# Six input buffers, mix tiles of two units, and the last fifteen units transposed by the crossbar, in a gated token-mixing kernel

## The chip, the core and the metric

The kernel runs on one core of a Trainium2 chip. The core has a matrix engine (TensorE: PE for its matmuls, PEld for its weight loads), a vector engine (DVE), an activation engine (ACT), a general engine (POOL) and a queue engine (SP), each with its own in-order stream of instructions, and 16 DMA engines that they share. The metric is the device time of one execution in microseconds; the median of several executions is compared.

## The reference

```python
x_prev[:, 1:, :] = x[:, :-1, :]              # x_prev is 0 for the first token of a batch
xv = x * time_mix_v + x_prev * (1 - time_mix_v)
xr = x * time_mix_r + x_prev * (1 - time_mix_r)
v = xv @ value_weight
r = xr @ receptance_weight
out = (sigmoid(r) * v) @ output_weight
```

`x` has 16 batches of 2048 tokens with 256 features in float32; the four weights used here are 256 x 256 or vectors of 256. The key branch of the reference does not reach the output.

## The kernel before

**Units.** A batch of 2048 tokens is cut into 4 units of 512 tokens, which makes 64 units. Unit g belongs to batch g // 4. A batch from number 2 on is loaded with one DMA from POOL's queue (`load`, L109), which turns float32 into bfloat16, into a buffer `x_bf` of 128 partitions, 16 tokens each. There are five such buffers.

**Transposes.** The products need the features on the partitions. `transposes(i)` does this for unit i with 8 matmuls against an identity (L203) into `ps_t`, and ACT copies the result to `xt` (L219). A batch's `xt` has 17 slots of 128 columns: slots 1 to 16 hold its tokens, and slot 0 holds the predecessors of slot 1's tokens, that is slot 16 moved by one column. The last unit of a batch is therefore transposed first, and `wrap_slots` copies slot 16 to slot 0 on DVE (L413). Some units go another way: `by_dma` (L182) has SP issue one transposing DMA, which sends `x_bf` through the crossbar into `xt`. In the kernel before these are one unit in batch 4, one in batch 8 (`MID_T`), one in batch 12, and the three whole batches 13, 14 and 15. The one in batch 12 waits for the last input load besides its own.

**Mixing.** The weights are scaled by the mixing vector once, so that a mixed operand is c * x_prev + x. The product with c goes to DVE (L255), POOL (L265) and, late in the kernel, ACT (L495), half of the features at a time; DVE does the sums (L277). From unit 10 on a product covers two units. The results stand in `mix`, in two buffers of one batch each.

**The loop.** For each unit g, PE does 4 matmuls into `psum_r` (L285, called R here), then possibly the transposes of unit g + 6, then 4 matmuls into `psum_v` (V), then 8 matmuls of the output of unit g - 1 into `psum_o` (L309, O). ACT takes the sigmoid of `psum_r` (L516), copies the transposes, and copies `psum_o` to `o_sb` (L341). DVE multiplies sigmoid and `psum_v` to `z_sb` (L553). `psum_r`, `psum_v` and `psum_o` have one buffer each, so V of unit g + 1 waits until DVE has read V of unit g. SP stores two units at a time (L319, L344); the order of work on each engine is the order in which the program writes it.

**Stages.** `NU - BYDMA` is 51: units 1 to 50 are transposed on PE except for the two of `MID_T`. `CROSS` is 45, from where PE transposes nothing. From there one product of each pair of units goes to ACT instead of DVE. The transposing DMAs of batches 13, 14 and 15 are issued when g is 45, 47 and 51. The first units are prepared with 38 filler matmuls (`warm_up`), with unit 0 transposed from float32 in two halves, and with two transposes more for slot 0 of unit 0. The load of batch b + 4 is issued when batch b begins to be transposed.

The lines that the change touches are the constants at L48 to L68, `load`, `transposes`, `first_transposes`, `mixed`, `output`, `advance` and the loop from L502 on.

Of the kernel before, what the change touches and what calls it, by code (L numbers as in the profile page):

```python
# [8 lines left out]
FP32 = mybir.dt.float32  # L9
# [6 lines left out]
def kernel(  # L16
# [35 lines left out]
    LOOK = 6  # L52
    BYUNIT = 2
    H = UJ // 2
    BYDMA = 3 * UB + 1
    CROSS = NU - BYDMA - LOOK
    MID_T = (4 * UB, 8 * UB)
    START_T = [1, 3, 5, 6, 7, 9, 11, 12]
    AHEAD = 6
    PAIRS = 10  # L60
    WARM = 21
    WARM1 = 2
    WARM2 = 15

    consts = ctx.enter_context(tc.tile_pool(name="consts", bufs=1))
    xpool = ctx.enter_context(tc.tile_pool(name="xpool", bufs=5))
    xtpool = ctx.enter_context(tc.tile_pool(name="xtpool", bufs=3))
    mixpool = ctx.enter_context(tc.tile_pool(name="mixpool", bufs=2))  # L68
    zpool = ctx.enter_context(tc.tile_pool(name="zpool", bufs=3))
    opool = ctx.enter_context(tc.tile_pool(name="opool", bufs=3))  # L70
    ps_t_pool = ctx.enter_context(tc.tile_pool(name="ps_t", bufs=2, space=bass.MemoryType.PSUM))
# [28 lines left out]
    def load(b):  # L100
        if b not in x_bf:
            x_bf[b] = xpool.tile([P, J, D], BF16, name="x_bf")
        if b < BYUNIT:
            for e in range(UB):
                nc.gpsimd.dma_start(
                    out=x_bf[b][:, e * UJ : (e + 1) * UJ, :], in_=unit_rows(x, b, e)[:, 0]
                )
            return
        return nc.gpsimd.dma_start(out=x_bf[b], in_=rows(b), max_dma_last_dim=2048)  # L109

    x_unit = opool.tile([P, 3, UJ, D], FP32, name="o_sb")
    tm_rows = consts.tile([2 * KO, P], FP32)
# [62 lines left out]
        nc.vector.tensor_scalar(out=c_sb, in0=c_sb, scalar1=-1.0, scalar2=None, op0=ALU.add)  # L175

    coefficients()
    warm_up(WARM1)

    def by_dma(b, lo, hi, after=None):  # L180

# [7 lines left out]
    def transposes(i):  # L189

        b, e = divmod(i, UB)
        if b > 0 and e == 0 and b not in xt:
            new_xt(b)
        if b >= BYUNIT:
            e = (e - 1) % UB
        if UB * b in MID_T and e == 2:
            return
        j0 = 1 + e * UJ + (e if b < BYUNIT else 0)
        if b < BYUNIT or e == UB - 1:
            late_copies.append((b, e))  # L200

        def one(ps, jj, ko, src, idn):
            nc.tensor.transpose(  # L203
                out=ps[:, jj], in_=src[:, jj, ko * P : (ko + 1) * P], identity=idn
            )

        if i in (1, 2):
            for ko in range(KO):
                ps = ps_t_pool.tile([P, UJ, P], FP32, name="ps_t")
                for jj in range(UJ):  # L210
                    one(ps, jj, ko, x_unit[:, i], ident_f)
                nc.scalar.copy(out=xt[b][:, j0 : j0 + UJ, ko, :], in_=ps)
            return
        ps = ps_t_pool.tile([P, UJ, KO, P], BF16, name="ps_t")
        src = x_bf3 if b == 0 else x_bf[b][:, e * UJ : (e + 1) * UJ, :]
        for jj in range(UJ):
            for ko in range(KO):
                one(ps[:, :, ko], jj, ko, src, ident)
        nc.scalar.copy(out=xt[b][:, j0 : j0 + UJ], in_=ps)  # L219

    def first_transposes():
        def half(h, pool, name):
            ps = pool.tile([P, UJ, KO, P], FP32, name=name)
            for jj in range(H):
                for ko in range(KO):
                    nc.tensor.transpose(
                        out=ps[:, jj, ko],
                        in_=x_unit[:, 0, h * H + jj, ko * P : (ko + 1) * P],
                        identity=ident_f,
                    )  # L230
            nc.scalar.copy(out=xt[0][:, 1 + h * H : 1 + h * H + H], in_=ps[:, 0:H])

        pl = ps_t_pool.tile([P, KO, P], FP32, name="ps_t")
        for ko in range(KO):
            nc.tensor.transpose(
                out=pl[:, ko, 0:P], in_=x_unit[:, 0, UJ - 1, ko * P : (ko + 1) * P], identity=ident_f
            )
        nc.vector.tensor_copy(out=xt[0][:, 0, :, 1:P], in_=pl[:, :, 0 : P - 1])
        half(1, ps_r_pool, "psum_r")
        half(0, ps_v_pool, "psum_v")  # L240

# [5 lines left out]

    def mixed(piece):
        b, m, lo, hi = piece
        return mix[b][:, m, lo // P : hi // P]  # L250

    def scale(piece, kos=(0, 1)):
        b, m, _, _ = piece
# [27 lines left out]
    def project(ps, g, m, lo=0, hi=TU):  # L281
        b, e = divmod(g, UB)
        for mo in range(KO):
            for ko in range(KO):
                nc.tensor.matmul(  # L285
                    out=ps[:, mo, :],
                    lhsT=w_bf[:, m, ko, mo * P : (mo + 1) * P],
                    rhs=mix[b][:, m, (e * TU + lo) // P : (e * TU + hi) // P, ko],
                    start=(ko == 0),
                    stop=(ko == KO - 1),  # L290
                )
# [37 lines left out]
    def output(g, z):  # L329
# [1 line left out]
        if e == 0:  # L331
            o_sb[b] = opool.tile([P, J, D], FP32, name="o_sb")
        j0 = e * UJ
        if g >= NU - 3:
            for h, (pool, name) in enumerate([(ps_o_pool, "psum_o"), (ps_t_pool, "ps_t")]):
                out_part(pool, name, z, b, e, h * H, H, nc.scalar.copy, nc.sync)
            return
        ps = ps_o_pool.tile([P, UJ, D], FP32, name="psum_o")
# [3 lines left out]
        if b < BYUNIT:  # L342
            if e % 2 == 1:
# [1 line left out]
                    out=unit_rows(out, b, e - 1, 2),  # L345
                    in_=o_sb[b][:, j0 - UJ : j0 + UJ, :].rearrange("p (e j) d -> p e j d", j=UJ),
                )
        elif b == B - 1:
            store(nc.sync, b, j0, j0 + UJ)
        elif e % 2 == 1:  # L350
            store(nc.sync, b, j0 - UJ, j0 + UJ)
# [33 lines left out]
        out_part(ps_t_pool, "ps_t", z_sb, b, e, 3, 1, by_dve, nc.sync)  # L385

    def tile_for(b):
        if b not in mix:
            mix[b] = mixpool.tile([P, 2, J, KO, P], BF16, name="mix")

    def pieces(g):

        b, e = divmod(g, UB)
        tile_for(b)
        return [(b, m, e * TU, (e + 1) * TU) for m in range(2)]

    def wrap_slots(piece, one=None):
# [22 lines left out]
    def advance(limit):  # L420
        nonlocal tnext, last_load
        while tnext <= min(limit, NU - 1):
            b, e = divmod(tnext, UB)
            if b == 1 and e > 0:
                load(b + e + 1)
            elif b > 1 and e == 0 and b + 4 < B:
                last_load = load(b + 4)
            if tnext < NU - BYDMA:
                transposes(tnext)
            tnext += 1  # L430

    first_transposes()
    tile_for(0)
    for ko in range(KO):
        nc.vector.tensor_scalar(
            out=w_prev[:, ko, :],
# [62 lines left out]
                scale=c_sb[:, m, ko : ko + 1],  # L499
            )  # L500

    z_prev = None  # L502
    for g in range(NU - 1):
        ps_r = ps_r_pool.tile([P, KO, TU], FP32, name="psum_r")
        if g == 0:
# [8 lines left out]
            project(ps_r, g, 0)  # L514
        s_sb = zpool.tile([P, KO, TU], BF16, name="s_sb")
        nc.scalar.activation(out=s_sb, in_=ps_r, func=ACT.Sigmoid)  # L516
        if g == CROSS - 1:
            by_dma(B - 4, 2 * UJ, 3 * UJ, last_load)
        advance(START_T[g] if g < len(START_T) else g + LOOK)
        for b in range(B - 3, B):  # L520
            if g == max(UB * (b - 2) - 1, CROSS):
                new_xt(b)
                late_copies.append((b, UB - 1))
                by_dma(b, 0, J)
        if g + 2 * UB in MID_T:
            b = g // UB + 2
            new_xt(b)
            by_dma(b, 2 * UJ, 3 * UJ)
        for p in products.get(g + 1, []):
            if g >= CROSS and p[0][1] == 1:  # L530
                scale_act(p[0], (0,))
        for p in [q for q, _ in products[g]] + pooled[g]:
            last_unit_of = p[3] // TU - 1
# [4 lines left out]
        if g == 1:  # L538
            scale_act(pieces(2)[1], (1,))
        for p, kos in products[g]:  # L540
            if not (g - 1 >= CROSS and p[1] == 1):
                scale(p, kos)
        for p in sums[g]:
            last = add(p)
# [10 lines left out]
            scale_pool(p, last)  # L555
        for p in held[g]:
            add(p)
        if z_prev is not None:
            output(g - 1, z_prev)
        if g == 1:  # L560
            advance(4)
        z_prev = z_sb
    last_unit(NU - 1)


# [28 lines left out]
```

## Time and profile before

| what | value |
|---|---|
| median of 4 runs | 207.0 us (206.49 to 207.71) |
| the profiled execution's own time | 206.64 us |
| its span, from first to last instruction | 204.9 us |
| PE busy | 197.3 us (96%) |
| DVE busy | 189.1 us (92%) |
| ACT busy | 179.3 us (88%) |
| POOL busy | 86.0 us (42%) |
| input loads of a whole batch | 14, 932 ns to issue, 27.3 us median to landing (13.5 to 40.3) |
| stores of two units | 30, 7.5 us median to landing |
| granted TensorE clock | 0.9 or more of full speed in every slice |

A busy share is the sum of the durations of an engine's instructions, where overlaps count once; neighbouring instructions of one engine overlap by about 0.1 us, so a duration is longer than the distance to the next start. A row of the timeline gives start, duration, engine, line, operation, output and input, and in brackets the idle time before it and what ended it. Times below are counted from the span's start. An instruction that issues a DMA occupies its queue for the duration in its row; the transfer lands later.

### The profile page before, as it was taken

The numbers are of one execution on the slowest core, as the hardware profiler recorded it, in microseconds if no ns is written. First come the engines' busy times: TensorE is split into PE (matmuls) and PEld (weight loads), VectorE is DVE, ScalarE is ACT, GpSimd is POOL, SyncE is SP. The second block draws the span as 40 slices with busy tenths as digits, with TensorE's granted clock in tenths as the row PEclk, the third lists the DMA queues.
The fourth block names the chain that finished last, engine by engine and source line by source line (L and its number), as shares of the span: only waits on it lengthen the run. The fifth ranks groups of instructions, "written<-read, shape, count | busy, mean of one in ns | idle before, by whom it ended". The sixth has DMA issues, their size and how long they took to land.

```text
span 204.9 us, 3972 instructions
## 1 busy us (share of the span) xinstructions
PE 197.3 (96%) x1469; PEld 128.0 (62%) x1469; DVE 189.1 (92%) x308; ACT 179.3 (88%) x197; POOL 86.0 (42%) x109
## 2 busy tenths in 40 slices
PE   8999996999999999999999999999999999999992
PEld 7656664666666666666666666666655555555670
DVE  3899998999999999999999999999999999999962
ACT  3799897999899999999899999999988989898981
POOL 1864615253543545354264535434424444444200
PEclk9999999999999999999999999999999999999999
DMA  5999999999999999999999999999879999984385
GB/s 185 288 181 204 260 287 257 304 206 153 268 371 356 334 299 277 275 277 243 354 323 285 283 278 286 309 310 298 276 242 237 266 300 289 314 352 202 160 333 206
DMA packets 38379, 55.96 MB, mean 273 GB/s; under 512 B 16596, under 2 KB 32216, under 8 KB 35032
## 3 DMA queue, kind: packets, MB, share of 16 engines
q1 hardware_dynamic: 22656, 39.46, 56.0%
q0 software_dynamic: 15552, 16.12, 47.5%
q8 instruction: 11, 0.18, 0.3%
q10 hardware_dynamic: 152, 0.13, 0.2%
q14 instruction: 8, 0.07, 0.1%
HBM read 34.34 MB, written 33.55 MB: 331 GB/s over the span
## 4 chain that ended last, share of the span: by engine, by line
PE 70%; DMA 9%; ACT 8%; DVE 7%; issue 4%; POOL 1%; DVEq 0%; POOLq 0%
PE psum_v L285 20%; PE psum_o L309 19%; PE psum_r L285 17%; DMA x_bf<-in_x_dram 9%; PE ps_t L203 9%; ACT s_sb L516 5%; DVE z_sb L553 4%; PE ps_t L144 2%; ACT mix L495 2%; ACT o_sb L341 1%; DVE mix L277 1%; PE psum_r L299 1%; DVE mix L255 1%; POOL mix L265 1%; PE ps_t L309 1%
## 5 line engine op out<-in xcount | busy, mean ns | idle before, releaser
L265 POOL TENSOR_SCALAR mix<-xt,c_sb 128x1024 bf16<-128x1024 bf16 (+1 forms) x55 | 61.0, 1109 | 93.3 <-DVE mix L277 87.3
L553 DVE TENSOR_TENSOR z_sb<-s_sb,psum_v 128x1024 bf16<-128x1024 bf16 x63 | 76.7, 1218 | 4.1 <-PE psum_v L285 2.3
L277 DVE TENSOR_TENSOR mix<-mix,xt 128x1024 bf16<-128x1024 bf16 x112 | 77.3, 695 | 2.0
L341 ACT COPY o_sb<-psum_o 128x1024 f32<-128x1024 f32 x61 | 62.0, 1017 | 15.0 <-PE psum_o L309 14.8
L285 PEld LDWEIGHTS <-w_bf 128*128 128x128 bf16 x516 | 48.6, 98 | 38.4 <-issue 3.3
L285 PE MATMUL psum_v<-mix,w_bf 128*128 128x512 bf16 (+1 forms) x256 | 65.2, 377 | 0.7 <-DVE mix L277 0.2
L516 ACT ACTIVATE s_sb<-psum_r 128x1024 bf16<-128x1024 f32 x63 | 65.2, 1035 | 0.2 <-PE psum_r L299 0.2
L309 PE MATMUL psum_o<-wo_bf,z_sb 128*128 128x256 bf16 x498 | 64.8, 273 | 0.0
L285 PE MATMUL psum_r<-mix,w_bf 128*128 128x512 bf16 (+1 forms) x252 | 64.2, 377 | 0.0
L309 PEld LDWEIGHTS <-z_sb 128*128 128x128 bf16 x512 | 49.9, 98 | 19.8 <-DVE z_sb L370 0.8
L219 ACT COPY xt<-ps_t 128x1024 bf16<-128x1024 bf16 x41 | 41.6, 1026 | 0.8 <-PE ps_t L203 0.8
L203 PEld LDWEIGHTS <-x_bf 128*128 128x128 bf16 x368 | 24.0, 98 | 12.3 <-DMA x_bf<-in_x_dram 2.8
L203 PE MATMUL ps_t<-ident,x_bf 128*128 128x128 bf16 x368 | 27.6, 219 | 1.8 <-DMA x_bf<-in_x_dram 1.8
L255 DVE TENSOR_SCALAR mix<-xt,c_sb 128x1024 bf16<-128x1024 bf16 (+1 forms) x53 | 25.3, 486 | 0.0
L109 POOL DMA_DIRECT2D x_bf<-in_x_dram x14 | 13.1, 934 | 0.0
L277 DVE TENSOR_TENSOR mix<-mix,xt_first 128x1024 bf16<-128x1024 bf16 x15 | 10.2, 687 | 0.2 <-POOL mix L265 0.2
L495 ACT ACTIVATE mix<-xt,c_sb 128x1024 bf16<-128x1024 bf16 x8 | 9.2, 1149 | 0.0
L265 POOL TENSOR_SCALAR mix<-xt_first,c_sb 128x512 bf16<-128x512 bf16 x6 | 4.2, 697 | 7.8 <-DVE xt_first L413 7.8
L255 DVE TENSOR_SCALAR mix<-xt_first,c_sb 128x512 bf16<-128x512 bf16 x22 | 6.6, 348 | 0.2
L219 ACT COPY xt_first<-ps_t 128x1024 bf16<-128x1024 bf16 x5 | 5.1, 1018 | 0.0
L144 PE MATMUL ps_t<-zeros 128*128 128x128 bf16 x38 | 3.8, 275 | 1.0 <-DVE zeros L87 1.0
L144 PEld LDWEIGHTS <-zeros 128*128 128x128 bf16 x38 | 3.2, 125 | 1.0 <-DVE zeros L87 1.0
(65 smaller groups left out, 45.7 us busy)
## 6 DMA issues: line engine op xcount, KB each, us to landing
out_dram<-o_sb SPq DMA_DIRECT2D x30, 1024.0 KB, 7.5
x_bf<-in_x_dram POOLq DMA_DIRECT2D x14, 1024.0 KB, 27.3
x_bf<-in_x_dram POOLq DMA_DIRECT2D x5, 256.0 KB, 7.3
o_sb<-in_x_dram SPq DMA_DIRECT2D x2, 512.0 KB, 4.6
out_dram<-o_sb SPq DMA_DIRECT2D x4, 256.0 KB, 2.1
o_sb<-in_x_dram SPq DMA_DIRECT2D x2, 256.0 KB, 3.0
out_dram<-o_sb SPq DMA_DIRECT2D x1, 512.0 KB, 2.8
out_dram<-o_sb SPq DMA_DIRECT2D x3, 128.0 KB, 2.1
```

The costliest lines, as they stand in the source:

```text
L109: return nc.gpsimd.dma_start(out=x_bf[b], in_=rows(b), max_dma_last_dim=2048)
L203: nc.tensor.transpose(out=ps[:, jj], in_=src[:, jj, ko * P : (ko + 1) * P], identity=idn)
L219: nc.scalar.copy(out=xt[b][:, j0 : j0 + UJ], in_=ps)
L255: nc.vector.tensor_scalar(out=mixed(piece)[:, :, ko], in0=xt[b][:, slots(piece), ko], scalar1=c_sb[:, m, ko : ko + 1], scalar2=None, op0=A ...
L265: op = nc.gpsimd.tensor_scalar(out=mixed(piece)[:, :, 1], in0=xt[b][:, slots(piece), 1], scalar1=c_sb[:, m, 1:2], scalar2=1.0, op0=ALU.mul ...
L277: return nc.vector.tensor_tensor(out=mixed(piece), in0=mixed(piece), in1=xt[b][:, slots(piece, 1)], op=ALU.add)
L285: nc.tensor.matmul(out=ps[:, mo, :], lhsT=w_bf[:, m, ko, mo * P : (mo + 1) * P], rhs=mix[b][:, m, (e * TU + lo) // P : (e * TU + hi) // P, ...
L309: nc.tensor.matmul(out=ps[:, slot, :], lhsT=z[:, ko, jj * P : (jj + 1) * P], rhs=wo_bf[:, ko, :], start=(ko == 0), stop=(ko == KO - 1),)
L341: nc.scalar.copy(out=o_sb[b][:, j0 : j0 + UJ, :], in_=ps)
L495: nc.scalar.activation(out=mixed(piece)[:, :, ko], in_=xt[b][:, slots(piece), ko], func=ACT.Copy, scale=c_sb[:, m, ko : ko + 1],)
L516: nc.scalar.activation(out=s_sb, in_=ps_r, func=ACT.Sigmoid)
L553: nc.vector.tensor_tensor(out=z_sb, in0=s_sb, in1=ps_v, op=ALU.mult)
```

## The change

Sizes and counts: `BYDMA` goes from 13 to 15, so units 49 to 63 go by the crossbar and `CROSS` becomes 43; `MID_T` is gone, and PE transposes units 1 to 48 without exception. There are six input buffers instead of five, and the load of batch b + 5 is issued where that of b + 4 was. Each load is cut into pieces of 2048 float32 numbers instead of 512. `mix` has three buffers of two units instead of two of four.

Order: batch 12's transposing DMA now covers three units and is issued at g = 43, directly ahead of that of batch 13; those of batches 14 and 15 stay at g = 47 and 51. Slot 0 of batches 13 to 15 is filled by a DMA from SP (three of them) instead of a copy on DVE. From g = 44 on the output of unit g - 2 stands between R and V; before, the output of unit g - 1 stood after V. At g = 61 two outputs are written out. Units 56 to 59 are stored one by one, unit 60 in two halves, as units 61 and 62 were.

Start: seven filler matmuls and the two transposes for slot 0 of unit 0 are gone; DVE makes that slot from the first half's result.

```diff
-    BYDMA = 3 * UB + 1
+    BYDMA = 3 * UB + 3
     CROSS = NU - BYDMA - LOOK
-    MID_T = (4 * UB, 8 * UB)
+    FREE = CROSS
+    LATE_O = CROSS
-    WARM1 = 2
-    WARM2 = 15
+    WARM2 = 10
-    xpool = ctx.enter_context(tc.tile_pool(name="xpool", bufs=5))
+    xpool = ctx.enter_context(tc.tile_pool(name="xpool", bufs=6))
-    mixpool = ctx.enter_context(tc.tile_pool(name="mixpool", bufs=2))
+    mixpool = ctx.enter_context(tc.tile_pool(name="mixpool", bufs=3))
...
-        return nc.gpsimd.dma_start(out=x_bf[b], in_=rows(b), max_dma_last_dim=2048)
+        return nc.gpsimd.dma_start(out=x_bf[b], in_=rows(b), max_dma_last_dim=8192)
...
-    warm_up(WARM1)
...
-        if UB * b in MID_T and e == 2:
-            return
...
+            if h == 1:
+                nc.vector.tensor_copy(out=xt[0][:, 0, :, 1:P], in_=ps[:, H - 1, :, 0 : P - 1])
             nc.scalar.copy(out=xt[0][:, 1 + h * H : 1 + h * H + H], in_=ps[:, 0:H])
-        pl = ps_t_pool.tile([P, KO, P], FP32, name="ps_t")
-        for ko in range(KO):
-            nc.tensor.transpose(
-                out=pl[:, ko, 0:P], in_=x_unit[:, 0, UJ - 1, ko * P : (ko + 1) * P], identity=ident_f
-            )
-        nc.vector.tensor_copy(out=xt[0][:, 0, :, 1:P], in_=pl[:, :, 0 : P - 1])
...
-            mix[b] = mixpool.tile([P, 2, J, KO, P], BF16, name="mix")
+            mix[b] = mixpool.tile([P, 2, 2 * UJ, KO, P], BF16, name="mix")
...
-            elif b > 1 and e == 0 and b + 4 < B:
-                last_load = load(b + 4)
+            elif b > 1 and e == 0 and b + 5 < B:
+                if b == 2:
+                    load(6)
+                last_load = load(b + 5)
...
-        if g == CROSS - 1:
-            by_dma(B - 4, 2 * UJ, 3 * UJ, last_load)
+        if g == CROSS:
+            by_dma(B - 4, 0, 3 * UJ, last_load)
...
             if g == max(UB * (b - 2) - 1, CROSS):
                 new_xt(b)
-                late_copies.append((b, UB - 1))
                 by_dma(b, 0, J)
-        if g + 2 * UB in MID_T:
-            b = g // UB + 2
-            new_xt(b)
-            by_dma(b, 2 * UJ, 3 * UJ)
+                shifted = b
+        if LATE_O < g < NU - 2:
+            output(g - 2, z_prev2)
...
-        if z_prev is not None:
+        if z_prev is not None and not LATE_O <= g < NU - 3:
             output(g - 1, z_prev)
...
+        if shifted is not None and g == max(UB * (shifted - 2), CROSS + 1):
+            nc.sync.dma_start(
+                out=xt[shifted][:, 0, :, 1:P], in_=xt[shifted][:, J, :, 0 : P - 1]
+            )
```

## The prediction, made before the changed kernel was run

> **What bounds the kernel now.** I read the page's busy shares first (PE 96%, DVE 92%, ACT 88%: no engine has much room), then ACT's timeline, because the sigmoid (L516) starts when R of its unit is done and so marks each unit, then the rows of PE, DVE and SP where the distance between sigmoids departs from the rest.
>
> From unit 10 on, units with transposes on PE follow each other every 3.05 us (sigmoids at 43.57, 46.61, 49.66). The chain gives R, V and O 0.86, 0.86 and 0.87 us, and 8 transposes advance PE by 0.45: 3.04. Here **PE is the bound**. Units without transposes take 2.60 in the middle (52.71 to 55.31). Two places are worse than PE's own work.
>
> First, unit 7, whose sigmoid comes at 32.43 and whose successor's at 37.03. PE's and DVE's timelines there:
>
> ```profile
> 31.08 1.03 PE L285 MATMUL psum_r<-mix,w_bf 128*128 128x512 bf16 x4
> 33.73 0.62 PE L203 MATMUL ps_t<-ident,x_bf 128*128 128x128 bf16 x8 [1.62 <-DMA x_bf<-in_x_dram]
> ...
> 33.90 0.69 DVE L277 TENSOR_TENSOR mix<-mix,xt 128x1024 bf16<-128x1024 bf16 x1
> 35.32 1.22 DVE L553 TENSOR_TENSOR z_sb<-s_sb,psum_v 128x1024 bf16<-128x1024 bf16 x1 [0.73 <-PE psum_v L285]
> ```
>
> PE stands 1.62 us for batch 3's load; DVE only 0.73, because it was behind.
>
> Second, everything after the last transposes (sigmoid of unit 46 at 151.91, of unit 62 at 195.11): 16 units in 43.20, or 2.70 each, where PE needs 2.60. ACT's and DVE's timelines:
>
> ```profile
> 157.60 1.03 ACT L516 ACTIVATE s_sb<-psum_r 128x1024 bf16<-128x1024 f32 x1
> 158.51 1.15 ACT L495 ACTIVATE mix<-xt,c_sb 128x1024 bf16<-128x1024 bf16 x1
> 159.55 1.01 ACT L341 COPY o_sb<-psum_o 128x1024 f32<-128x1024 f32 x1
> 160.44 1.04 ACT L516 ACTIVATE s_sb<-psum_r 128x1024 bf16<-128x1024 f32 x1
> ...
> 161.52 1.22 DVE L553 TENSOR_TENSOR z_sb<-s_sb,psum_v 128x1024 bf16<-128x1024 bf16 x1 [0.30 <-ACT s_sb L516]
> ...
> 162.79 1.02 PE L285 MATMUL psum_v<-mix,w_bf 128*128 128x512 bf16 x4
> ```
>
> The reader is to see a ring: mix and copy hold ACT, the sigmoid starts late, z waits for it, and the next V waits for z, since `psum_v` is single.
>
> **Start: 0.** Gone are two float32 transposes (0.43 us of PE) and seven fillers. They stand ahead of the first real matmul at 6.04, which waits for `w_prev` on DVE (5.61, after 0.66 idle for the receptance weight's landing). If fewer fillers let PE's clock fall, the next 3.4 us (the early fillers ran 107 ns apart from 0.99 until about 4.4, then 56) would run at half speed: +1.7. The gap is only about 0.5 us, so I take 0. The other end, should a little come free, is -0.2.
>
> **Load: -1.3.** Of the trace's packet records on the loads' queue, those of 512, 1024 and 2048 bytes (as written) last 60, 98 and 173 ns: a line, 22 ns + 0.0735 per byte. A piece of 2048 numbers writes 4096 bytes: 323, against 4 x 98 = 392. A load falls from 1024 x 98 / 16 = 6.3 us of the 16 engines to 256 x 323 / 16 = 5.2. Batch 2 lands at 23.2 and batch 3 at 33.7, with DMA shares of 1.15 to 1.2, so full. Two loads save 2.2, and longer load packets should take a larger part beside stores (172 ns): batch 3 lands at about 30, before PE asks at 32.1. The Trainium skill (DMA: Bandwidth & Descriptors, Specifications) speaks against this: transfers from 512 bytes on already reach line rate. Then nothing is won and the stall stays. The line through three measured sizes says otherwise for this cast load; the size itself is extrapolated. The ends are 0 and -1.6; with PE's wait gone DVE is late next: z of unit 7 gains 0.73, later z's about 1.0, and PE can use up to 1.5 since V tolerates a late z. I take -1.3.
>
> The sixth buffer only issues loads 12 us earlier. After 34 us no transpose waits for a load, so that costs and gains nothing, except that all loads should have landed before 140 (the last landed at 146.2). POOL's issues get shorter, which is hidden in its 58% idle time. The mix tiles' reuse is five units after the last reader, as before: 0.
>
> **Middle: +0.9.** Units in batches 4 and 8 return to PE: 2 x 0.45, all on PE's path. The two crossbar transfers they replace ran beside loads (12.9 and 13.6 us to landing) and held SP 1.3 and 2.6, but nobody waited for them.
>
> **End: -2.0.** From the sigmoid of unit 43 (143.21) to that of 62 the time before is 51.90. After: 19 units x 2.60 = 49.4, without transposes. One bubble: O of unit 42 moves behind R of 44, so R 44 follows V 43 directly and waits 0.16 for the sigmoid. The order R, O, V gives ACT 0.87 more before z needs the sigmoid: behind copy and mix (0.91 each for sigmoid and copy, 1.04 for mix, in starts) the next sigmoid ends 3.9 after R of the unit before, and its V only 4.3 after. On DVE, starts lie 1.14 (z), 0.60 (sum) and 0.40 (product) apart, so z's are 2.74 apart with a product and 2.34 without, 2.54 in the mean: it keeps up with 2.60, barely. Ideal: -2.3. For jitter, 0.015 per unit, I take **-2.0**. The other end is the cadence of before, 2.70: -0.6. The displaced O's come back at unit 61, so their work is counted. Three DVE copies (0.13 each in starts) are hidden. The tail from 195 on is the same work: 0; more, smaller stores land in idle DMA.
>
> **Crossbar chain: +0.6, the largest doubt.** SP's timeline, and the landings of the last three:
>
> ```profile
> 149.94 7.16 SPq L182 DMA_TRANSPOSE xt<-x_bf  x1
> 157.19 0.53 SPq L319 DMA_DIRECT2D out_dram<-o_sb  x1
> 157.89 7.27 SPq L182 DMA_TRANSPOSE xt<-x_bf  x1
> 165.25 1.02 SPq L319 DMA_DIRECT2D out_dram<-o_sb  x2
> 166.44 9.29 SPq L182 DMA_TRANSPOSE xt<-x_bf  x1
> ...
> DMA to landing us min/median/max: 8.8/8.8/8.8
> ...
> DMA to landing us min/median/max: 10.8/10.8/10.8
> ...
> DMA to landing us min/median/max: 11.0/11.0/11.0
> ```
>
> In times of before (moved by what is won earlier): the store of unit 41 lets batch 12 start at 143.9. Three units, at three quarters of the rows, issue for 5.4 and land at 150.5 to 152.3; DVE's product at g = 46 wants them by 151.2, and a z may be late by 0.4 without harm. Batch 13 starts at 149.3 and lands at 158.1 to 160.1. Then comes what is new: SP waits for that landing to issue slot 0's DMA, and behind it stand the next store and batch 14. No row shows such a small copy inside SBUF; a 128 KB store (2.1 us) is nearest, the ends are 0.3 and 3.3 (the quickest transposing DMA). I take 2.1. Batch 14 starts at about 160, lands at 169 to 171, its slot 0 at 171.3 to 173.5, wanted at 172.1 (+0.4). Batch 15: start 170 to 172, slot 0 at 181 to 185, wanted at 182.5 (+0.4). In the fast case nothing waits; in the slow case the stalls at 12, 14 and 15 add up to about 3.7. The middle of the landings is some 0.6 late. By the skill (same page, Latency and other measured facts: 261 GB/s for a transposing DMA) a batch of 1 MB would take 4.0 us and never be late; the rows, 95 to 119 GB/s from issue to landing, decide. The held stores' buffers are not needed for 12 us or more.
>
> **Sum.** -1.3 + 0.9 - 2.0 + 0.6 = -1.8: profiled execution 206.64 to 204.8, span 204.9 to 203.1. That execution lies 0.4 below the median of 207.0, so the forecast of the median is 207.0 - 1.8 = **205.2**.
>
> **Rivals.**
> - *The crossbar chain decides* (slower). SP's waits serialize transfer, slot 0 and next transfer; landings of 11 us give +3.7 in place of +0.6: 207.0 - 2.4 + 3.7 = 208.3. For it: two of three landings at 10.8 and 11.0, and batches must follow every 10.4. Against it: loads are gone by then and batches 12 and 13 start earlier. It decides from an interval above 10.4 us between transposing DMAs of 14 and 15. Chance 0.18.
> - *The larger pieces bring nothing*: the stall of unit 7 stays. 207.0 + 0.9 - 2.0 + 0.6 = 206.5. Chance 0.15.
> - *DVE bounds the end*: the new order only moves the wait, cadence 2.70. 207.0 - 1.3 + 0.9 - 0.6 + 0.6 = 206.6. For it: DVE's 92%. Chance 0.12.
> - The forecast as summed, 203.8 to 206.0: 0.55.
>
> **How the numbers follow.** What can be told from no change is 0.5%, so 206.0 to 208.0 counts as the same. Of the forecast nearly all is below 206.0, with a little of the two middle rivals: faster 0.57. They and two fifths of the chain rival: same 0.29. Rest of the chain rival and the clock: slower 0.14. Range: below, all gains whole and no late transfer, 203.6; above, into the chain rival, 207.7.
>
> **What would show it.** Right: no PE row with a wait for `x_bf` near 32; sigmoids 3.05 apart throughout the middle, with no 2.60; 2.60 to 2.63 apart from unit 44 to 61; no wait of DVE, ACT or POOL for a transposing DMA or slot 0 above 1 us. Wrong: load packets near 390 ns; sigmoids still 2.70 apart at the end with DVE waiting for nothing; DVE's product at g = 46, 54 or 58 waiting for DMA by more than 1 us; matmuls after 6 us at twice the distance of before.

## The result, and the profile after

The changed kernel takes 206.21 us in the median of 41 executions (205.62 to 207.52), the kernel before 207.35 in 62 (205.55 to 209.63). The ratio of executions run side by side is 0.996, with a 95% interval from 0.9949 to 0.9972: faster by 0.4%, or about 0.8 us (1.14 by the medians), where 1.8 was forecast. The time lies inside the range. The profiled executions took 206.64 before and 205.75 after, with spans of 204.9 and 204.0.

The budget below is read from ACT's timeline: the start of the sigmoid of unit g is called s(g). The start of one execution can differ by more than a microsecond from that of the next, so a second profile of the kernel before stands beside the first.

| stretch | before | before, second profile | after | forecast of the change | after - before (first profile) |
|---|---|---|---|---|---|
| start to s(0) | 8.95 | 9.58 | 9.50 | 0 | +0.55 |
| s(0) to s(7) | 23.48 | 23.54 | 23.30 | 0 | -0.18 |
| s(7) to s(8) | 4.60 | 4.50 | 3.20 | -1.3 | -1.40 |
| s(8) to s(43) | 106.18 | 106.18 | 107.08 | +0.9 | +0.90 |
| s(43) to s(62) | 51.90 | 51.92 | 51.05 | -2.0 + 0.6 | -0.85 |
| s(62) to the span's end | 9.8 | 9.9 | 9.9 | 0 | +0.1 |

**Unit 7.** PE's timeline after, and DVE's z of unit 7, where PE had stood 1.62 us:

```profile
31.45 1.03 PE L279 MATMUL psum_r<-mix,w_bf 128*128 128x512 bf16 x4
32.31 0.61 PE L200 MATMUL ps_t<-ident,x_bf 128*128 128x128 bf16 x8
33.16 1.02 PE L279 MATMUL psum_v<-mix,w_bf 128*128 128x512 bf16 x4 [0.24 <-DVE z_sb L548]
...
35.02 1.20 DVE L548 TENSOR_TENSOR z_sb<-s_sb,psum_v 128x1024 bf16<-128x1024 bf16 x1
...
DMA to landing us min/median/max: 15.4/15.4/15.4
```

The last line is that of batch 3's load. The transposes follow R with no wait. Batch 3's load was issued at 15.2 and landed 15.4 later, at 30.6 (33.7 before). A wait of 0.24 for DVE's z is what is late next. Why the load came earlier is seen best in the DMA view of the stretch from 23.5 to 26.5 us, while the first store runs. Columns: queue, packets, MB, share of the 16 engines; q0 is the loads' queue, q1 SP's. First the kernel before, then the changed one:

```profile
q1 hardware_dynamic: 188, 0.77, 68.1%
q0 software_dynamic: 198, 0.20, 39.8%
```

```profile
q0 software_dynamic: 99, 0.41, 66.7%
q1 hardware_dynamic: 101, 0.41, 36.9%
```

Both have about as many packets of one queue as of the other: the engines take them by turns. Before, a load packet is 1,024 bytes and a store packet 4,096, so the loads get a fifth of the bytes (0.20 of 0.97 MB). Now both are 4,096 and the loads get half.

**The end.** ACT, DVE and PE at a place where nothing is late, the new order R, O, V:

```profile
161.79 1.02 ACT L513 ACTIVATE s_sb<-psum_r 128x1024 bf16<-128x1024 f32 x1 [0.61 <-PE psum_r L279]
162.71 1.01 ACT L335 COPY o_sb<-psum_o 128x1024 f32<-128x1024 f32 x1
163.60 1.16 ACT L491 ACTIVATE mix<-xt,c_sb 128x1024 bf16<-128x1024 bf16 x1
...
163.77 1.21 DVE L548 TENSOR_TENSOR z_sb<-s_sb,psum_v 128x1024 bf16<-128x1024 bf16 x1
...
164.19 1.04 PE L303 MATMUL psum_o<-wo_bf,z_sb 128*128 128x256 bf16 x8
165.06 1.03 PE L279 MATMUL psum_v<-mix,w_bf 128*128 128x512 bf16 x4
```

The ring is open: z no longer waits for the sigmoid (0.30 before), V no longer for z, and ACT has idle time of its own (0.61). Steps alternate between 2.86 and 2.34, the forecast 2.60 in the mean.

**Batch 12.** SP's timeline and three landings: those of batch 12, of batch 14, and of the first slot-0 copy.

```profile
143.73 10.94 SPq L181 DMA_TRANSPOSE xt<-x_bf  x2
156.62 0.70 SPq L558 DMA_DIRECT2D xt<-xt  x1
...
158.15 7.14 SPq L181 DMA_TRANSPOSE xt<-x_bf  x1
...
DMA to landing us min/median/max: 7.8/7.8/7.8
...
DMA to landing us min/median/max: 10.4/10.4/10.4
...
DMA to landing us min/median/max: 2.1/2.1/2.1
```

Issue and landing of batch 12 fell where they were put (143.9 and 150.5 to 152.3 in the prediction, 143.73 and 151.5 here), the first slot-0 copy took the 2.1 us assumed for it (the next two 2.4 and 2.8), and nobody waited for batches 13 to 15. But batch 12 was waited for. POOL's, DVE's and PE's timelines:

```profile
147.33 1.12 POOL L259 TENSOR_SCALAR mix<-xt,c_sb 128x1024 bf16<-128x1024 bf16 x1 [1.63 <-DVE mix L271]
151.72 3.00 POOL L259 TENSOR_SCALAR mix<-xt,c_sb 128x1024 bf16<-128x1024 bf16 x2 [3.28 <-DMA xt<-x_bf]
...
151.63 0.49 DVE L249 TENSOR_SCALAR mix<-xt,c_sb 128x1024 bf16<-128x1024 bf16 x1 [0.18 <-DMA xt<-x_bf]
...
153.77 2.09 DVE L271 TENSOR_TENSOR mix<-mix,xt 128x1024 bf16<-128x1024 bf16 x2
...
155.31 1.04 PE L279 MATMUL psum_r<-mix,w_bf 128*128 128x512 bf16 x4 [0.38 <-DVE mix L271]
```

DVE's product waited 0.18. POOL's product on the same slots could have begun at 148.44 and waited 3.28; then two of POOL's products stood in a row (3.00), DVE's sums came late (153.77), and s(46) to s(48) took 5.97.

### The profile page after: what moved, and what is told of

It is laid out like the page before. It is cut to its first block, busy times and chain, and to the rows that moved or that the text cites. A ratio compares the mean times of both kernels' runs of the same rounds, so it can differ in the third digit from the quotient of the medians.

```text
span 204.0 us, 3968 instructions
## 1 busy us (share of the span) xinstructions
PE 196.7 (96%) x1460; PEld 127.6 (63%) x1460; DVE 188.6 (92%) x304; ACT 180.0 (88%) x199; POOL 84.3 (41%) x109
## 4 chain that ended last, share of the span: by engine, by line
PE 73%; DVE 10%; DMA 7%; ACT 3%; issue 3%; POOL 1%; SPq 1%; DVEq 0%; POOLq 0%
PE psum_v L279 22%; PE psum_o L303 21%; PE psum_r L279 21%; PE ps_t L200 8%; DVE mix L271 4%; DMA xt<-x_bf 4%; DVE z_sb L548 3%; DMA w_f<-in_value_weight_dram 3%; DVE mix L249 2%; ACT s_sb L513 1%; ACT o_sb L335 1%; POOL mix L259 1%; PE ps_t L303 1%; ACT mix L491 1%; ACT xt L216 0%
## 5 line engine op out<-in xcount | busy, mean ns | idle before, releaser
L259 POOL TENSOR_SCALAR mix<-xt,c_sb 128x1024 bf16<-128x1024 bf16 (+1 forms) x55 | 61.8, 1123 | 92.9 <-DVE mix L271 83.9
L271 DVE TENSOR_TENSOR mix<-mix,xt 128x1024 bf16<-128x1024 bf16 x112 | 78.1, 704 | 1.9
L335 ACT COPY o_sb<-psum_o 128x1024 f32<-128x1024 f32 x60 | 61.1, 1018 | 7.8 <-PE psum_o L303 7.7
L249 DVE TENSOR_SCALAR mix<-xt,c_sb 128x1024 bf16<-128x1024 bf16 (+1 forms) x52 | 23.5, 459 | 0.2 <-DMA xt<-x_bf 0.2
L109 POOL DMA_DIRECT2D x_bf<-in_x_dram x14 | 10.5, 752 | 0.0
L491 ACT ACTIVATE mix<-xt,c_sb 128x1024 bf16<-128x1024 bf16 x9 | 10.4, 1160 | 0.0
L144 PE MATMUL ps_t<-zeros 128*128 128x128 bf16 x31 | 3.1, 281 | 1.0 <-DVE zeros L87 1.0
L209 ACT CAST xt_first<-ps_t 128x512 bf16<-128x512 f32 x4 | 2.1, 588 | 1.6 <-PE ps_t L200 1.6
```

The lines of the kernel that those rows point to most:

```text
L249: nc.vector.tensor_scalar(out=mixed(piece)[:, :, ko], in0=xt[b][:, slots(piece), ko], scalar1=c_sb[:, m, ko : ko + 1], scalar2=None, op0=A ...
L259: op = nc.gpsimd.tensor_scalar(out=mixed(piece)[:, :, 1], in0=xt[b][:, slots(piece), 1], scalar1=c_sb[:, m, 1:2], scalar2=1.0, op0=ALU.mul ...
L271: return nc.vector.tensor_tensor(out=mixed(piece), in0=mixed(piece), in1=xt[b][:, slots(piece, 1)], op=ALU.add)
L335: nc.scalar.copy(out=o_sb[b][:, j0 : j0 + UJ, :], in_=ps)
L491: nc.scalar.activation(out=mixed(piece)[:, :, ko], in_=xt[b][:, slots(piece), ko], func=ACT.Copy, scale=c_sb[:, m, ko : ko + 1],)
```

## The experiments

"Changed kernel" is the kernel after. Ratios are to the kernel before, run beside on the same chip; the changed kernel's own is 0.996.

**1. The start of before put back.** The two float32 transposes for slot 0 and all fillers return.

```diff
-    WARM2 = 10
+    WARM1 = 2
+    WARM2 = 15
...
+    warm_up(WARM1)
...
-            if h == 1:
-                nc.vector.tensor_copy(out=xt[0][:, 0, :, 1:P], in_=ps[:, H - 1, :, 0 : P - 1])
...
+        pl = ps_t_pool.tile([P, KO, P], FP32, name="ps_t")
...
+        nc.vector.tensor_copy(out=xt[0][:, 0, :, 1:P], in_=pl[:, :, 0 : P - 1])
```

> The changed kernel with the start of before: two transposes for slot 0 of unit 0 in a bank of their own, 38 fillers. Theory (ACT's copy of the first half waits for DVE's read of the same bank, which delays the first matmul): PE's wait for ACT at the first matmul (0.52 us) is gone, the first sigmoid comes near 9.0 instead of 9.5, and the kernel is 0.3 to 0.5 us faster than the changed one (about 205.8). Rival (the start's delay is absorbed later, or is a chance of one profile): the sigmoids of units 4 to 8 stand where they stood in the changed kernel and the time is unchanged within 0.2 us.

Measured: 206.70 us (22 executions), ratio 0.9978 (0.996 to 0.9995). So the new start is not seen to be slower; by the medians it gains 0.5, but the two intervals overlap.

Over the 19 profiles at full clock, of all kernels, s(0) lies between 8.95 and 12.98, and two things move it. The first is the landing of unit 1's input, whose DMA is issued at 2.15 in all of them: PE transposes unit 1 between the two halves of R of unit 0. It landed between 6.91 and 9.29, and in 15 of the 19 s(0) comes 2.03 to 2.09 after it, with the old start and with the new (before 6.91 and 8.95, after 7.46 and 9.50). That is the +0.55 of the budget.

The second is PE's rate. PE's timeline of the kernel before, and below it that of the first profile of experiment 2, which has the new start:

```profile
6.04 0.64 PE L299 MATMUL psum_r<-xt_first,w_prev 128*128 128x512 bf16 x2
6.55 0.61 PE L299 MATMUL psum_r<-xt_first,w_bf 128*128 128x512 bf16 x2
7.00 1.05 PE L203 MATMUL ps_t<-ident_f,o_sb 128*128 128x128 f32 x8
```

```profile
6.94 1.06 PE L293 MATMUL psum_r<-xt_first,w_prev 128*128 128x512 bf16 x2
7.79 1.06 PE L293 MATMUL psum_r<-xt_first,w_bf 128*128 128x512 bf16 x2
8.65 1.70 PE L200 MATMUL ps_t<-ident_f,o_sb 128*128 128x128 f32 x8
```

Here a pair of matmuls takes 1.06 us in place of 0.64 and 0.61, the sign that the prediction named, and s(0) comes 3.11 after the landing. Of the 16 profiles with the new start three are like this: 3.11, 2.83 (the fourth of experiment 5) and 3.68 (the third of experiment 12, where PE stands idle for 2.05 until the landing and then has a granted clock of 0.50 from 10 to 12 us). That is 0.8 to 1.6 us lost; in the other 13 it is 0.2 at most. None of the three profiles with the old start is like this, which is too few to say that the fillers prevent it, and the timing shows no gain from them.

**2. Batch 12's transfer one unit earlier.** Nothing else is changed.

```diff
-        if g == CROSS:
+        advance(START_T[g] if g < len(START_T) else g + LOOK)
+        if g == CROSS - 1:
             by_dma(B - 4, 0, 3 * UJ, last_load)
-        advance(START_T[g] if g < len(START_T) else g + LOOK)
```

> The changed kernel with batch 12's transposing DMA issued one unit earlier, at g = 42 behind the transposes and ahead of the store of unit 41. Theory (only batch 12's transfer is late; POOL's 3.3 us wait for it costs PE about 0.95): POOL's wait for the transposing DMA disappears, the sigmoids of units 46 to 50 are 2.60 apart in the mean, and the kernel is 0.8 to 1.0 us faster than the changed one (about 205.3). Rival (the chain as a whole is what binds): the wait moves to batch 13, 14 or 15 and less than 0.4 us is won.

Measured: 205.50 us (8 executions), ratio 0.9926 (0.9895 to 0.9958). SP's and POOL's timelines of this kernel:

```profile
139.26 5.97 SPq L181 DMA_TRANSPOSE xt<-x_bf  x1
...
151.50 1.12 POOL L259 TENSOR_SCALAR mix<-xt,c_sb 128x1024 bf16<-128x1024 bf16 x1 [1.43 <-PE psum_v L279]
```

The issue comes 4.5 us earlier, POOL's wait for the transfer is gone, s(46) to s(48) is 5.22, and s(43) to s(62) is 50.10 in place of 51.05. Batch 12's late landing cost 0.95 in the profile and about 0.7 in the time.

**3. The same once more,** for a better interval.

> The changed kernel with only batch 12's transfer issued one unit earlier, once more, since its first timing rested on 8 executions. Theory (the transfer's lateness costs 0.7 to 1.0): 205.2 to 205.7, ratio 0.990 to 0.994, units 43 to 62 in 50.1. Rival (that timing was favoured by chance, the transfer is worth nothing): 206.2, ratio 0.996.

Measured: 205.56 us (12 executions), ratio 0.9918 (0.9883 to 0.9953), and 50.10 again.

**4. The output's old place.** The output of unit g - 1 stands behind V again.

```diff
-    LATE_O = CROSS
+    LATE_O = NU
...
-        if z_prev is not None and not LATE_O <= g < NU - 3:
+        if z_prev is not None:
```

> The changed kernel with the output of unit g - 1 behind V to the end, as before. Theory (the order R, O, V takes ACT's late sigmoid out of the ring): the distance of sigmoids from unit 50 to 60 goes from 2.60 back to about 2.69 and the kernel is slower by 1.0 to 1.7 us (about 207.5). Rival (DVE has become lighter by the slot copies and sets 2.60 in either order): within 0.4 us of the changed kernel.

Measured: 207.51 us (22 executions), ratio 1.0023 (1.0003 to 1.0044), s(43) to s(62) 51.85. The new order is worth 1.3 us in the time. Past batch 12 the cadence shows it: s(50) to s(60) takes 26.75 here and 26.00 in the changed kernel. Batch 12's transfer is late in this kernel too, as POOL's timeline shows:

```profile
152.53 3.00 POOL L259 TENSOR_SCALAR mix<-xt,c_sb 128x1024 bf16<-128x1024 bf16 x2 [3.21 <-DMA xt<-x_bf]
```

So the new order is not what makes it late. The steps from s(47) to s(51) add up to 11.38, where the same four steps of the next period take 10.78: an estimate of 0.6 us for the delay with the old order. With the new order it costs 0.95, and where the transfer is in time (experiment 2) the stretch falls from 51.90 to 50.10, by 1.80.

**5. Load pieces of before.** The changed kernel with pieces of 512 numbers.

```diff
-        return nc.gpsimd.dma_start(out=x_bf[b], in_=rows(b), max_dma_last_dim=8192)
+        return nc.gpsimd.dma_start(out=x_bf[b], in_=rows(b), max_dma_last_dim=2048)
```

> The changed kernel with loads in pieces of 512 numbers, as before; six buffers stay. Theory (the larger pieces alone bring batch 3 in time): batch 3 lands after 33 us again, PE waits about 1.6 us for it, the step from unit 7 to 8 goes from 3.2 back to 4.6, and the kernel is slower by 1.2 to 1.6 us (about 207.6). Rival (the sixth buffer and the earlier issue do it): no PE wait, time unchanged. Third possibility: also the last load lands late, past 140, and batch 12's transfer waits for it, which would add up to 2 us more.

Measured: 207.47 us (14 executions), ratio 1.0013 (0.9991 to 1.0035), 1.26 above the changed kernel. Yet the profile showed no stall at unit 7 (step 3.35, batch 3 landed at 31.5). So three more profiles of it were taken.

> A second profile of the changed kernel with load pieces of 512 numbers. Theory (the larger pieces are worth 1.3 us because they take the stall at unit 7 away): in this profile the sigmoids of units 7 and 8 are 4.2 to 4.7 us apart, batch 3 lands after 33.0 us, and the first small-pieces profile, with no stall, was one of its quicker executions. Rival (the stall belongs to the kernel before, not to the piece size, and the small pieces lose their 1.3 us elsewhere): 3.0 to 3.4 us apart again.

> A third profile of the changed kernel with pieces of 512 numbers. The packet records say that loads move 63 KB per us beside a store and stores 256, so batch 3's load either ends just before the second store's packets start (31.5 in the two profiles so far, no stall) or some 3 us later (34.2 in the kernel with crossbar units, whose instructions are the same until then). Theory (a knife's edge, met or missed by chance): either a step of 3.35 with a landing at 31 to 32, or one of 4.4 to 4.9 with a landing at 34 to 35, and the stall in one of this and the next profile at least. Rival (the stall needs the crossbar units in the program): 3.35 in both.

> A fourth profile of the same kernel, with the same two theories: 3.35 and a landing at 31 to 32, or 4.4 to 4.9 and a landing at 34 to 35.

The second (207.89) and fourth (207.59) had steps of 3.35, the third (207.38) 4.38. PE's timeline in the third, and the landings of batch 3 in the third and the fourth:

```profile
31.82 1.04 PE L279 MATMUL psum_r<-mix,w_bf 128*128 128x512 bf16 x4
34.11 0.62 PE L200 MATMUL ps_t<-ident,x_bf 128*128 128x128 bf16 x8 [1.26 <-DMA x_bf<-in_x_dram]
...
DMA to landing us min/median/max: 18.6/18.6/18.6
```

```profile
DMA to landing us min/median/max: 14.7/14.7/14.7
```

The knife's edge stands, as the packet records of the third and fourth show. Loads move about 200 KB per us alone and 63 beside a store. In the third profile the second store's packets begin at about 29.5 us; by 30.0 the packets of 2.00 of the 2.10 MB of batches 2 and 3 had begun, and the rest crawled: landing at 34.1. In the fourth the second store begins at about 30.7, and by 30.0 load packets of 2.16 MB had begun, some of them batch 4's: landing at 31.4. All profiles, by piece size and start:

| load pieces | s(0) below 10 | s(0) from 10 on |
|---|---|---|
| 512 or 1024 numbers | 7 profiles, 6 with a step of 4.4 to 4.9 | 4 profiles, none |
| 2048 numbers | 3 profiles, none | 5 profiles, none |

In these profiles a late start lets the loads finish before the second store begins. So with small pieces an execution lost either at the start or, in 6 of 7, at unit 7; with large ones only at the start. The four profiles have s(0) to s(62) longer than the changed kernel's by 0.25 to 1.32, less in the mean than the 1.26 that was timed.

**6. A second look at the kernel before.**

> The kernel before, unchanged, for a second profile. Question: is the wait for batch 3's load at unit 7, and the first sigmoid at 8.95 us, a property of this kernel or of one execution? Theory (the stall is in nearly every execution, since the loads fill the DMA engines): PE again waits 1 to 2 us for batch 3 and the step from unit 7 to 8 is about 4.6. Rival (it comes and goes with how the first DMAs land): the step is 3.2 to 3.4 here and the whole time lies near 206.

Measured: 207.37 us, step 4.50 at unit 7.

**7. Large pieces in the kernel before.** Pieces of 2048 numbers, nothing else.

```diff
-        return nc.gpsimd.dma_start(out=x_bf[b], in_=rows(b), max_dma_last_dim=2048)
+        return nc.gpsimd.dma_start(out=x_bf[b], in_=rows(b), max_dma_last_dim=8192)
```

> The kernel before with the one edit of loads in pieces of 2048 numbers. Theory (larger pieces are worth about 1.2 us by themselves, as undoing them in the changed kernel cost 1.2): about 206.0, ratio 0.994, no PE wait for batch 3, the last load lands before 140. Rival (they only pay together with the sixth buffer): within 0.3 us of before.

Measured: 214.14 us in the median of five executions, ratio 1.0351 (1.0314 to 1.0388): 7 us slower where a gain was expected. A sixth, the profiled one, had a granted clock of 0.66 and took 297.91; in it batch 4's crossbar transfer landed after 12.8 us and nobody waited for it, so it does not show the reason. The next experiment makes one likely; for this kernel it is not shown.

**8. The middle's crossbar units put back,** with large pieces.

```diff
+    MID_T = (4 * UB, 8 * UB)
...
-        if b > 0 and e == 0:
+        if b > 0 and e == 0 and b not in xt:
...
+        if UB * b in MID_T and e == 2:
+            return
...
+        if g + 2 * UB in MID_T:
+            b = g // UB + 2
+            new_xt(b)
+            by_dma(b, 2 * UJ, 3 * UJ)
```

> The changed kernel with the two crossbar units of batches 4 and 8 put back, beside the loads; batch 12 still has three. PE transposes two units less. Theory (PE's work returned to the middle costs 0.9, and a crossbar transfer beside loads harms nobody): 0.8 to 0.9 us faster than the changed kernel, about 205.3, sigmoids of units 13 and 14 and of 29 and 30, or thereabouts, 2.60 apart. Rival (it delays loads or stores so that something waits): unchanged or slower, with a wait on DMA in the middle.

Measured: 219.65 us, ratio 1.0599 (1.0562 to 1.0635). SP's, POOL's, DVE's and PE's timelines, and the landing of batch 4's unit:

```profile
37.14 7.81 SPq L182 DMA_TRANSPOSE xt<-x_bf  x1
...
DMA to landing us min/median/max: 30.1/30.1/30.1
...
68.14 0.75 POOL L110 DMA_DIRECT2D x_bf<-in_x_dram  x1 [12.04 <-DMA xt<-x_bf]
...
70.13 0.69 DVE L274 TENSOR_TENSOR mix<-mix,xt 128x1024 bf16<-128x1024 bf16 x1 [10.37 <-POOL mix L262]
...
72.01 1.86 PE L282 MATMUL psum_v<-mix,w_bf 128*128 128x512 bf16 x4 [9.70 <-DVE z_sb L555]
```

One unit's transfer, which landed in 12.9 us before, takes 30.1. POOL's next load (L110) is to fill the input buffer that this transfer still reads, and waits for it 12.04; POOL's product stands behind that load, DVE waits for POOL, PE for DVE. In the kernel before, where the transfer landed at 54.5, POOL came to its load only at 55.4. The DMA view of 47 to 53 us, first of the kernel before, then of this one:

```profile
q0 software_dynamic: 734, 0.74, 88.1%
q1 hardware_dynamic: 735, 0.19, 40.7%
```

```profile
q0 software_dynamic: 289, 1.12, 96.1%
q1 hardware_dynamic: 289, 0.09, 12.1%
```

In both, one load packet goes for each packet of 256 bytes of the transposing DMA. With load packets of 4,096 bytes that leaves 289 transposing packets in 6 us instead of 735, of 1,024 that the unit has.

**9. The same with batch 12 early.** The edits of experiments 2 and 8 together.

> The changed kernel with both: batch 12's transfer one unit earlier, and the two crossbar units of batches 4 and 8 back. Theory (the two parts are independent and add): 206.2 - 0.8 - 0.9 = 204.5, ratio to before about 0.987. Rival (they are two names for one slack): no better than the better one of them, 205.3.

Measured: 218.67 us, ratio 1.0567 (1.0532 to 1.0602). The step from unit 16 to 17 is 17.30; s(43) to s(62) is 50.09. So the middle alone costs the 13 us.

**10. The same with pieces of 1024 numbers** (packets of 2,048 bytes, 173 ns), to see whether the effect grows with the packet.

```diff
-        return nc.gpsimd.dma_start(out=x_bf[b], in_=rows(b), max_dma_last_dim=8192)
+        return nc.gpsimd.dma_start(out=x_bf[b], in_=rows(b), max_dma_last_dim=4096)
```

> The kernel with batch 12's transfer issued earlier, the crossbar units in batches 4 and 8 put back, and load pieces of 1024 numbers (2,048-byte packets, 173 ns by the packet records). Theory of packets by turns: 64 transposing packets per engine times 18 + 173 ns make about 12 us of packets for batch 4's unit, landing some 8 us earlier than with the 4,096-byte packets, so the stall at unit 16 to 17 falls from 14 us to between 3 and 7, and the time to 207 to 212. Rival (a threshold between 1,024 and 2,048 bytes, no gradual effect): packets of about 20 us as with 4,096 bytes and a time of 218 to 220. If no wait at all is left there, 204.8.

Measured: 206.38 us (10 executions), ratio 0.9983 (0.9949 to 1.0017). Landing, DVE's and PE's timelines:

```profile
DMA to landing us min/median/max: 16.8/16.8/16.8
...
62.33 0.69 DVE L274 TENSOR_TENSOR mix<-mix,xt 128x1024 bf16<-128x1024 bf16 x1 [2.45 <-POOL mix L262]
...
64.21 1.02 PE L282 MATMUL psum_v<-mix,w_bf 128*128 128x512 bf16 x4 [1.66 <-DVE z_sb L555]
```

The first to the last of the unit's transposing packets start 12.2 us apart, where turns give 64 x (18 + 173) ns = 12.2. The step from unit 16 to 17 is 4.87, a stall of 1.82: less than the 3 to 7 expected. The mechanism came out to the number, the cost did not.

**11. The middle's crossbar units with pieces of 512 numbers.** The edits of experiments 5 and 8 together.

> The changed kernel with load pieces of 512 numbers and with one crossbar unit each in batches 4 and 8, so the end's changes on the middle and load of before. Theory (each DMA engine takes packets by turns from the loads and from the transposing queue, so that the 19.6 us of the transposing packets are the price of the 4,096-byte load packets): the packets of batch 4's unit run about 8 us, POOL waits under 1 us for them, no sigmoid step above 5 us but perhaps that of unit 7, and the time is that of the small-pieces kernel less 0.9: 206.6, ratio 0.996 to 0.999. Rival (the sixth buffer's earlier loads or the mix tiles of two units make that transfer late, whatever the piece size): a stall of over 5 us at unit 16 to 17 stays, and the time is above 212.

Measured: 207.39 us (12 executions), ratio 1.0025 (1.0001 to 1.0048). Of the mechanism all came true: packets over 7.7 us, no wait of POOL for them, and the two steps of 2.60 back in the middle (s(8) to s(43) 106.19 against 107.08). The time did not: unit 7 stalled (4.62), and s(43) to s(62) was 52.37: batch 12's transfer, which waits for the last load, started only at 146.53.

**12. That with batch 12 early.** The edits of experiments 2, 5 and 8 together; one timing and two more profiles.

> The kernel with batch 12's transfer issued earlier, with the crossbar units in batches 4 and 8, and with pieces of 512 numbers. By the theory of packets by turns the transposing packets of batch 4's unit last about 8 us and nobody waits for them, while batch 3's load is robbed by the stores again: 205.5 (earlier transfer, large pieces, no crossbar units) + 1.3 in executions where unit 7 stalls - 0.9 = 205.5 to 206.0, ratio 0.992 to 0.996, and in the profile units 17 to 18 and 33 to 34 of 2.6 us. Rival (the crossbar units cost elsewhere what they save on PE, as the 207.4 of the kernel with the late transfer and small pieces suggests): 206.5 to 207, ratio 0.998 to 1.001.

> A second profile of the kernel with small pieces, earlier transfer and crossbar units, whose timed executions lie 2.4 to 3.5 us above its first profiled one (205.89). Theory (in the usual execution the start is early, s0 near 9.7, the stores rob batch 3's load, and the crossbar transfer of batch 4, which waits for batch 4's load behind it, is late besides): a step of 4.4 to 4.9 at unit 7 and another stall of 1 to 3 us at unit 16 to 18, total 208 to 209.5. Rival (the first profile is the usual case and the timed ones lost their time in the end's transfers): no stall at 16 to 18, steps of over 3 us between units 43 and 61.

> A third profile of the same kernel, with the same two theories. Should it again be one near 205.9 with s0 near 11, the excess of the timed executions stays open.

Measured: 208.65 us in the median of 7, ratio 1.0079 (1.0053 to 1.0106), though the first of them, the profiled one, took 205.89. The second and third profiles are of 207.94 and 207.46. In the second, the one with an early start (9.49), SP's and POOL's timelines:

```profile
145.55 3.62 SPq L182 DMA_TRANSPOSE xt<-x_bf  x1
...
173.75 3.00 POOL L262 TENSOR_SCALAR mix<-xt,c_sb 128x1024 bf16<-128x1024 bf16 x2 [3.44 <-DMA xt<-xt]
```

Batch 12's transfer was placed as in experiment 2 but starts at 145.55 instead of 139.26, because it waits for the last load: the last load packet ends at 145.0 here, at 132.9 in experiment 2. All later transfers are late in turn, slot 0 of batch 14 by 3.44, and s(43) to s(62) takes 53.05. No stall came at unit 16 to 18, so that half of the first theory fell. The first and third profiles, with starts of 11.1 and 13.0, had 50.10 at the end. This shows one way to lose 3 us, not that it is what the timed executions lost; that stays open.

**13. ACT's copy of the first half ahead of DVE's slot-0 copy,** on top of experiment 2.

```diff
+            nc.scalar.copy(out=xt[0][:, 1 + h * H : 1 + h * H + H], in_=ps[:, 0:H])
             if h == 1:
                 nc.vector.tensor_copy(out=xt[0][:, 0, :, 1:P], in_=ps[:, H - 1, :, 0 : P - 1])
-            nc.scalar.copy(out=xt[0][:, 1 + h * H : 1 + h * H + H], in_=ps[:, 0:H])
```

> The kernel with batch 12's transfer issued one unit earlier, and besides ACT's copy of the first half ahead of DVE's copy into slot 0, which read the same tile: the changed kernel's first matmul from the first half waited for that ACT copy, which waited 2.07 us for DVE's at the start. Theory (the earlier transfer is worth 0.7, a copy that no longer waits at the start a little more): 205.0 to 205.5, ratio 0.989 to 0.993. Rival (the start ends on the first transfers' landing, not on the copies): 205.5, the same as with the earlier transfer alone, first sigmoid at 9.5 or later.

Measured: 205.19 us (9 executions), ratio 0.9946 (0.9912 to 0.9979). ACT's copy starts at 4.57, waiting for PE alone, but s(0) is still at 10.31, again 2.04 after the landing of unit 1's input: the rival held. By the ratios it cannot be told from experiment 2. The version to keep is that of experiments 2 and 3.

## Why the prediction was right, and where it was wrong

The step that failed is the crossbar chain: it looked at the wrong reader of batch 12's transfer, and the late transfer cost 0.95 us where the whole chain was given 0.6. The end was 0.2 too hopeful. What is left of the miss, 0.4 to 0.7 us, lies in the start, which was put at 0, or in how often the load's gain comes; that stays open.

**Base and start (0).** In the profiles s(0) to s(62) fell by 1.51 (186.14 in the second profile of before to 184.63). The timing gives 0.8 by the ratio and 1.14 by the medians. The step weighed that fewer fillers let PE's clock fall, at +1.7, and put it at nothing because the gap was short. In three of 16 profiles matmuls did run at half rate at the start, and 0.8 to 1.6 us went (experiment 1), but putting the fillers back did not make the kernel faster. So the weighed branch exists, and its share in the median is not known.

**Load (-1.3).** Right where an execution starts early: packets of 4,096 bytes took 322 ns (forecast 323), batch 3 landed at 30.6 (about 30), the step fell by 1.40, and undoing this part alone cost 1.26 in the time. Of the two reasons given, the turns beside stores carry more than the shorter time per byte, which is only 323 against 392. The rule of the Trainium skill that was weighed (DMA: Bandwidth & Descriptors, Specifications: line rate from 512 bytes on) is not what these packets show: 10.4 bytes per ns at 1,024 and 12.7 at 4,096. It also speaks of the rate alone and so says nothing of shares; the same page's section on queues, rings and completion order says that an engine goes round its queues packet by packet, and the counts of 198 to 188 and 99 to 101 agree. What the step did not say is that the stall with small pieces comes only with an early start (experiment 5). An execution of the kernel before that starts late would then have no stall for the change to remove. Both profiles of that kernel start early, so this is not shown.

**Middle (+0.9).** Right to 0.01 in the profile. But the sentence beside it, "nobody waited for them", was true only of small load packets. Experiments 8 to 11 show that this part is the price of the larger pieces: with the crossbar units in the middle, pieces of 2048 numbers made the changed kernel 13 us slower, and pieces of 512 did not (experiments 11 and 5, 207.39 and 207.47). The two terms were added as if each could stand alone.

**End (-2.0).** The mechanism was right, the size not quite: -1.80 (51.90 to 50.10) where the transfer is in time. The bubble at unit 43 cost 0.41 (2.14 in place of 1.73), against the 0.16 of the sum, PE waiting 0.30 for the sigmoid; and at unit 61, where two outputs are written out, 0.27 more was lost: V ends, the first half of an output runs, and the second waits for `psum_o`.

**Crossbar chain (+0.6).** It measured +0.95, and in another place than forecast: all at batch 12, nothing at batches 14 and 15, for whose slot 0 the step held landings up to 1.4 and 2.5 us late possible. The step read "DVE's product at g = 46 wants them by 151.2, and a z may be late by 0.4 without harm". DVE was late by 0.18 just so; but the reader that mattered was POOL's product, ready at 148.44 and never named. Its wait of 3.28 put two of POOL's products in a row, and DVE's sums and PE's R behind them. Issuing the transfer 4.5 us earlier took this wait away, and with it 0.95 in the profile and about 0.7 in the time, twice.

**The sum.** From the forecast -1.8 to the -0.9 of the first pair of profiles: crossbar chain 0.35, end 0.2, start and its decay 0.37, tail 0.1, and the load's extra 0.1 the other way. That this pair agrees with the -0.8 of the timing is luck, because the first profile of before has the earliest start of all. The rival of the larger pieces bringing nothing and that of DVE as the bound fell. The chain rival did not decide the sign, but it was the right place to look. The kernel of experiment 2 comes to 205.5, near the 205.2 forecast for the change; it is another kernel, and this is no support for the forecast.

## What to carry to other kernels

When two queues share the DMA engines, look at the packet sizes of both: a larger packet on one is a smaller share for the other, and a transfer in small packets is then late by the count of its packets times the neighbour's packet time. For a transfer moved nearer to its use, list every engine that reads what it fills, and take the earliest time at which each is ready, not the one of the busiest engine; list also the load that will refill the buffer it reads. Before believing in a start or a stall seen in one profile, take a second of the same kernel: the two can hang together.

## What was not expected of the hardware

A unit's 1,024 transposing packets of 256 bytes took 8.4 and 7.7 us (kernel before, experiment 11) beside load packets of 1,024 bytes, 12.2 (experiment 10) beside 2,048, and 19.6 and 20.9 (experiments 8 and 9) beside 4,096. With next to no load packets beside them they took 2.7 and 3.8 (batch 8's unit in experiments 8 and 9). Packets by turns, 64 for each of 16 engines and 18 ns each beside 98, 173 and 322 ns, give 7.4, 12.2 and 21.8. The landing came 12.1 us after the issue in experiment 11, 16.8 in experiment 10 and 30.1 in experiment 8.
